# A two-layer hybrid backbone on one core: projections given out evenly between attention chunks, mask rows asked for three chunks ahead, the last MLP groups turned round

## The chip, the core and the metric

The kernel runs on one core of a Trainium2 chip. A core has five engines with instruction queues of their own: TensorE (PE, matrix products), VectorE (DVE), ScalarE (ACT), GpSimd (POOL) and SyncE (SP, which here issues nearly all DMAs). They meet through semaphores. The metric is device time in microseconds (us) of one execution; lower is better.

## What is computed

Two layers over 1024 latent tokens and 256 context tokens of width 1024, in fp32. Layer 0 mixes tokens by a short gated convolution, layer 1 by a bidirectional mLSTM with 8 heads. Each layer ends in an MLP with squared ReLU. The parts that matter here, cut:

```python
def _sqrelu_mlp(h, w1, w2):
    return jnp.square(jax.nn.relu(h @ w1)) @ w2

def body(carry, inp):                       # one chunk of 128 tokens of the mLSTM
    c_mat, n_vec, m = carry
    ...
    s = jnp.einsum('bhtd,bhsd->bhts', qc, kc) * jnp.exp(logd - m_t[..., None])
    w_inter = jnp.exp(inter - m_t)
    num = jnp.einsum('bhts,bhsv->bhtv', s, vc) + w_inter[..., None] * jnp.einsum('bhtd,bhdv->bhtv', qc, c_mat)
    den = jnp.sum(s, axis=-1) + w_inter * jnp.einsum('bhtd,bhd->bht', qc, n_vec)
    out = num / jnp.maximum(jnp.abs(den), jnp.exp(-m_t))[..., None]
    ...
    c_new = a[..., None, None] * c_mat + jnp.einsum('bhsd,bhsv->bhdv', kc * wk[..., None], vc)

def _mlstm_readout(h, o, norm_w, w_out):
    ...
    return (jax.nn.sigmoid(o) * h) @ w_out
```

The scan runs forwards and backwards in time, and both results are added.

## The kernel before

All large products are done in fp32 with operands split in a high and a low part, in three passes (`PASSES`); `split` (L109, L110) and `piece` (L122, L123) make the parts, each with one ScalarE cast and one VectorE subtraction. The order of work on each engine is made at build time by a list scheduler: an operation that stands earlier in the source has priority, but a later one may be put before it when the scheduler's own estimate says that the earlier one would wait. On the chip every engine then runs its list strictly in order.

**The MLP** (`mlp_up`, L488) uses a scheme with seven products for a two by two block product. For each of 16 steps `q` the weights are loaded and combined (`up_weights`), then `up_group` does a group of 84 products for the tokens of `A0` (384 of them a piece in layer 0, 256 in layer 1) and another for those of `A1`. A group's sums land in one tile `st7`, of which each pool has a single buffer (pool S1 for A0, pool M for A1), and one DMA stores it to `hid_d` (L469). `down_sums` (L471) loads the rows of the second weight matrix for a `k`, makes four differences on VectorE and stores them to `t_d`; it runs for `k = q - 2` at step `q`, and twice after the last step. `mlp_down` then reads `hid_d` (`hr`, L529; its pool lies over M's place), `w2` and `t_d`, casts and splits them, and does the down products `psd` (L536).

**The mLSTM** works through four pairs of heads (`Pair`, `j` 0 to 3). For a pair, `k`, `v` and `q` project the tokens (`psk`, `psv`, `psq`). `states` (L978) makes the state of each of 10 chunks (`pk`, `kk`, L982 to L998) and runs the recurrence over chunks on VectorE (L1002), for both directions at once. `attend` (L1006) then goes through 8 chunks for each head. A chunk's front (L1020 to L1040) makes the decay mask `Dm`: rows `nm_d` fetched to all partitions (one DMA per two chunks, two buffers), plus a triangular mask (L1026), exponential (L1032); it does the scores `po` (L1035) and their product with the mask, `pm` (L1039). A chunk's back multiplies with V and with the state (L1047, L1048, over `qw`, the queries times their decay, L1012) and normalises (L1052 to L1058) into `hb`. `out_gate` normalises a head (`rstd` on POOL, L241, L242, scaling L1070) and computes the gate (`pso`, sigmoid L1078); `read_out` transposes (`pth`, L1085), multiplies (L1087) and stores to `gd`, for all but the last two heads. `out_proj` (L353) loads those rows (`zt`), splits them (`zs`) and does the output products `op` (L371).

In the source the next pair's projections stand before `states` and `attend` of that pair as a whole; where they go on PE is the scheduler's choice.

Of the kernel before, what the change touches and what calls it, by code (L numbers as in the profile page):

```python
# [8 lines left out]
F32 = mybir.dt.float32  # L9
# [28 lines left out]
def hybrid_kernel(  # L38
# [449 lines left out]
    def mlp_up(l, As, sX, left, S1, acc):  # L488
# [317 lines left out]
    with ExitStack() as s1:  # L806
# [34 lines left out]
        class Pair:  # L841
# [12 lines left out]
            def k(self, groups, ps_pool=tp, tag="tp"):  # L854
                for t0, n in groups:
# [3 lines left out]

            def v(self, tiles):  # L860
                for t in tiles:
# [14 lines left out]
            def q(self, groups):  # L876
                w = load_w(wq[self.j])
                for t0, n in groups:
                    ps = tp.tile([P, 512], F32, tag="tp", name="psq")
                    mm_feat(ps[:, 0:n], w, t0, n)  # L880
# [4 lines left out]

        XG = ((256, 512), (768, 512))
        pair = Pair(0)
        pair.k(PG[0:2], acc, "acc")
        pair.v([0, 1, 2, 3, 4, 5, 7, 9])
        for f in pend:  # L890
            f(acc, "acc")
        pair.v([6, 8])
        gate_rows()
        pair.k(PG[2:])
        sT.close()
        with pool("gates", bufs=1, side="right") as gp:
# [60 lines left out]
            pair.q(XG)  # L957
            nxt = Pair(1)
            nxt.k(GROUPS)
# [18 lines left out]
        def states(pair):  # L978
            j = pair.j
            for c in range(NT):  # L980
# [9 lines left out]
                sb = 1 - c if c < NCT else NT + 1 - c  # L990
                for hh in range(2):
# [14 lines left out]
        def attend(pair, hh):  # L1006
            h = 2 * pair.j + hh
            kT, V, st = pair.kT, pair.V, sts[hh]
            qw = hp.tile([P, SEQ], F32, tag="qw", name="qw")
            for d, r in enumerate((lower, upper)):  # L1010
                nc.sync.dma_start(qw[r], w_d[d, h].partition_broadcast(64))
                nc.vector.tensor_mul(qw[r], qw[r], qz[hh * 64 : hh * 64 + 64, hh])  # L1012
            if pair.j < HEADS // 2 - 1:
                hb = hp.tile([P, 8, P], F32, tag="hb", name="hb")
            else:
                hb = pr.tile([P, 8, P], F32, tag="V" if hh else "kT", name="hb")
            ssq = small.tile([P, 8], F32, tag="ssq", name="ssq", bufs=4)
            Dm = {}

            def front(c):  # L1020
# [192 lines left out]
```

## Time and profile before

| | |
|---|---|
| time, median of 3 runs | 2582.22 us (2580.07 to 2582.91) |
| the profiled execution | 2577.89 us, of which the span of the profile is 2576.1 us |
| mean granted clock of TensorE | 0.989 of full |
| busy: PE, DVE, ACT, POOL | 97%, 64%, 44%, 4% of the span |
| chain that ended last | PE 53%, issue 30%, DVE 6%, DMA 6%, ACT 3%, POOL 2% |

PE is busy nearly always; that is a mean over stages, and "busy" says nothing of the clock. The part of the chain called issue is time in which an engine waited for nothing that the profile shows. The mLSTM stage is the stretch from about 1340 to 1860 us, the passages from the up to the down part of the MLP stand near 940 us (layer 0) and 2250 us (layer 1).

### The profile page before, as it was taken

Reading aid. Unit: us, or ns where it says so; the run is one execution under the profiler, and the core shown is the slowest. Engines: PE = TensorE matmul, PEld = TensorE weight load, DVE = VectorE, ACT = ScalarE, POOL = GpSimd, SP = SyncE. Lnnn points to the kernel's source line nnn. Section 1 sums busy time; section 2 is a strip of 40 time slices with the busy share of each in tenths; the row PEclk is TensorE's granted clock in tenths of the full one; section 3 lists DMA queues with packets and bytes.
Section 4 is the critical chain, followed back from the end, with each engine's and each line's share of the span. In section 5 each row is a group of like instructions: output and inputs, shape, how many; then the busy total and the mean of one; then the engine's idle time right before and its main releaser. Section 6 shows DMA issues by size and latency. Waiting matters only on the chain.

```text
span 2576.1 us, 38825 instructions
## 1 busy us (share of the span) xinstructions
PE 2488.1 (97%) x14520; PEld 2199.3 (85%) x14520; DVE 1651.6 (64%) x3058; ACT 1143.7 (44%) x2503; POOL 107.0 (4%) x229
## 2 busy tenths in 40 slices
PE   8999999999999999999999899999999999999998
PEld 5888887899999988888879788887789999978886
DVE  5777784687676664445864745546578787654565
ACT  5311112565445443334654444345456555444443
POOL 1000000100000000000111100000010000000010
PEclk9999999999999999999999899999999999999999
DMA  8456663436565676555751322222336777876675
GB/s 295 132 175 189 200 194 116 136 127 231 208 242 208 225 268 199 173 167 170 234 185 51 73 78 58 66 74 83 117 126 213 252 246 259 268 239 188 184 230 182
DMA packets 230207, 454.87 MB, mean 177 GB/s; under 512 B 17802, under 2 KB 109242, under 8 KB 230018
## 3 DMA queue, kind: packets, MB, share of 16 engines
q1 hardware_dynamic: 230018, 452.38, 54.2%
q8 instruction: 114, 1.87, 0.3%
q14 instruction: 75, 0.61, 0.1%
HBM read 326.78 MB, written 125.33 MB: 176 GB/s over the span
## 4 chain that ended last, share of the span: by engine, by line
PE 53%; issue 30%; DVE 6%; DMA 6%; ACT 3%; POOL 2%; DVEq 0%; POOLq 0%; SPq 0%; ACTq 0%
PE psd L536 12%; PE op L371 5%; PE psZ L433 4%; PE psW L433 4%; PE psX L433 4%; PE psv L865 3%; PE psc L129 3%; PE pso L129 3%; DMA Dm<-nm_d 3%; PE psb L129 3%; PE psu L129 3%; PE psY L433 2%; DMA mraw<-in_mod_w_dram 2%; PE psq L129 1%; DVE macc L220 1%
## 5 line engine op out<-in xcount | busy, mean ns | idle before, releaser
L536 PE MATMUL psd<-w,hp 128*128 128x512 f32 x3024 | 712.1, 397 | 10.8 <-ACT hp L530 10.8
L536 PEld LDWEIGHTS psd<-w,hp 128*128 128x128 f32 x3024 | 573.5, 190 | 145.7 <-ACT hp L530 11.9
L531 DVE TENSOR_TENSOR hp<-hr,hp 128x512 fp32r<-128x512 f32 (+1 forms) x226 | 169.4, 752 | 255.7 <-ACT hp L530 255.3
L530 ACT CAST hp<-hr 128x512 fp32r<-128x512 f32 (+1 forms) x226 | 151.1, 669 | 330.7 <-PE psd L536 278.0
L123 DVE TENSOR_TENSOR w<-raw,w 128x512 fp32r<-128x512 f32 x394 | 268.2, 685 | 40.9 <-ACT w L122 40.8
L122 ACT CAST w<-raw 128x512 fp32r<-128x512 f32 x394 | 242.5, 617 | 105.6 <-DMA raw<-in_w_dram 37.1
L433 PE MATMUL psX<-A,w 128*128 128x256 f32 (+1 forms) x1536 | 230.0, 298 | 2.2 <-ACT st L448 1.7
L433 PE MATMUL psZ<-A,w 128*128 128x256 f32 (+1 forms) x1536 | 226.8, 296 | 0.2 <-DVE st L452 0.2
L433 PE MATMUL psW<-A,w 128*128 128x256 f32 (+1 forms) x1536 | 226.8, 296 | 0.0
L433 PEld LDWEIGHTS psX<-A,w 128*128 128x128 f32 x1536 | 213.4, 189 | 3.4 <-ACT st L448 2.5
L433 PEld LDWEIGHTS psZ<-A,w 128*128 128x128 f32 x1536 | 211.9, 188 | 0.6 <-DVE st L452 0.5
L433 PEld LDWEIGHTS psW<-A,w 128*128 128x128 f32 x1536 | 211.8, 188 | 0.2 <-DVE st L454 0.2
L371 PE MATMUL op<-w,zs 128*128 128x512 f32 x864 | 206.1, 398 | 5.5 <-ACT zs L365 4.4
L371 PEld LDWEIGHTS op<-w,zs 128*128 128x128 f32 x864 | 162.5, 190 | 42.6 <-ACT zs L365 5.4
L463 ACT ACTIVATE st<-st 128x256 f32<-128x256 f32 (+1 forms) x192 | 85.2, 444 | 226.2 <-DVE st L454 159.0
L220 DVE SCALAR_TENSOR_TENSOR macc<-mraw,sil,macc 128x1024 f32<-128x1024 f32 x112 | 140.6, 1281 | 38.2 <-DMA mraw<-in_mod_w_dram 37.8
L109 ACT CAST w<-raw 128x1024 fp32r<-128x1024 f32 (+1 forms) x73 | 75.5, 1040 | 162.6 <-PE psc L129 61.6
L110 DVE TENSOR_TENSOR w<-raw,w 128x1024 fp32r<-128x1024 f32 (+1 forms) x73 | 87.8, 1209 | 78.7 <-ACT w L109 78.4
L865 PE MATMUL psv<-w,hT 128*128 128x256 f32 (+1 forms) x960 | 134.6, 294 | 0.5 <-ACT V L872 0.5
L865 PEld LDWEIGHTS psv<-w,hT 128*128 128x128 f32 x960 | 124.4, 192 | 1.1 <-ACT V L872 0.9
L433 PE MATMUL psY<-A,w 128*128 128x256 f32 (+1 forms) x768 | 116.0, 297 | 0.0
L129 PE MATMUL psc<-hT,w 128*128 128x512 f32 (+1 forms) x576 | 115.2, 352 | 0.6 <-DVE hT L279 0.4
(242 smaller groups left out, 3445.9 us busy)
## 6 DMA issues: line engine op xcount, KB each, us to landing
hid_d<-st SPq DMA_DIRECT2D x48, 896.0 KB, 5.1
mraw<-in_mod_w_dram SPq DMA_DIRECT2D x80, 512.0 KB, 4.0
raw<-in_w_dram SPq DMA_DIRECT2D x68, 512.0 KB, 3.8
hr<-hid_d SPq DMA_DIRECT2D x104, 320.0 KB, 3.7
rw<-in_w_dram SPq DMA_DIRECT2D x64, 512.0 KB, 5.7
raw<-t_d SPq DMA_DIRECT2D x128, 256.0 KB, 3.1
hr<-hid_d SPq DMA_DIRECT2D x122, 256.0 KB, 2.8
raw<-in_w_dram SPq DMA_DIRECT2D x96, 256.0 KB, 3.8
```

What stands on the lines that cost most here:

```text
L110: nc.vector.tensor_sub(w[1], src, w[0].bitcast(F32))
L122: nc.scalar.copy(w[:, 0], src)
L123: nc.vector.tensor_sub(w[:, 1], src, w[:, 0].bitcast(F32))
L129: nc.tensor.matmul(ps, w[a][:, k * P : (k + 1) * P], hold["hT"][:, k, b, t0 : t0 + n], start=(k == 0 and i == 0), stop=(k == KD - 1 and i ...
L220: nc.vector.scalar_tensor_tensor(ac[v], raw, s, ac[v], ALU.mult, ALU.add)
L371: nc.tensor.matmul(ps[h], zs[:, a, k, :], ws[k][b][:, h * 512 : (h + 1) * 512], start=(k == 0 and i == 0), stop=(k == KD - 1 and i == 2),)
L433: nc.tensor.matmul(ps, w[i][:, a, k * P : (k + 1) * P], A[:, PIECE[i], b, k, :], start=(first and k == 0 and j == 0), stop=(k == 3 and j = ...
L463: nc.scalar.activation(c, c, AF.Relu)
L530: nc.scalar.copy(h[:, 0], r)
L531: nc.vector.tensor_sub(h[:, 1], r, h[:, 0].bitcast(F32))
L536: nc.tensor.matmul(ps, h[:, a, o : o + P], w[:, b], start=(first and j == 0), stop=(last and j == 2))
L865: nc.tensor.matmul(ps[:, 0 : self.g], hold["hT"][:, k, a_, t * P : (t + 1) * P], self.wv[k // self.per][b_][:, k % self.per * self.g : (k ...
```

## The change

- `mlp_up`: steps 6 and 10 each do two `down_sums` in place of one, so that none is left after the last step. In the last step the group of A1 is done before that of A0.
- `k`, `v`, `q` and `out_gate` return lists of closures, one per PSUM tile (for `out_gate` half a tile). `Spread` calls them evenly over the steps of a loop. `states` gets, over its 10 steps, three `v` units of pair 1 for the first pair, later the gates and read-outs of the pair before (of its first head in the last pair). `attend` gets, over its 16 steps (both heads in one loop now), the other `v` and the `q` units of pair 1 (j = 0), the next pair's `k`, `v` and `q` (j = 1, 2), or the remaining gates, those of the last two heads too (j = 3).
- The mask rows come one chunk at a time (64 DMAs of 128 KB for 32 of 256 KB), in four buffers, asked for three chunks ahead, the first three before `states`; the mask is added in one operation per chunk, as many as before. The `qw` rows are asked for before `states`.
- After the last chunk only the read-outs of the last two heads are left.

```diff
@@ mlp_up
+            sums_due = 0
             for q in range(2, NQ):
                 w = up_weights(l, q, M)
-                down_sums(l, q - 2, M)
-                up_group(l, q, w, A0, n0, 0, S1, acc)
-                up_group(l, q, w, A1, n1, n0, M, acc)
-            down_sums(l, NQ - 2, M)
-            down_sums(l, NQ - 1, M)
+                for _ in range(2 if q in (6, 10) else 1):
+                    down_sums(l, sums_due, M)
+                    sums_due += 1
+                both = [(A0, n0, 0, S1), (A1, n1, n0, M)]
+                for A, n, c0, pl in both if q < NQ - 1 else both[::-1]:
+                    up_group(l, q, w, A, n, c0, pl, acc)
@@
+        class Spread:
+            def __init__(self, units, steps):
+                self.units, self.n, self.steps, self.done, self.i = units, len(units), steps, 0, 0
+
+            def __call__(self):
+                self.i += 1
+                while self.done * self.steps < self.i * self.n and self.done < self.n:
+                    self.units[self.done]()
+                    self.done += 1
@@ states
-        def states(pair):
+        def states(pair, step):
...
                 sb = 1 - c if c < NCT else NT + 1 - c
+                step()
                 for hh in range(2):
@@ attend
-                if c % 2 == 0:
-                    D2 = hp.tile([P, 2, 2 * P], F32, tag="Dm", name="Dm")
-                    nc.sync.dma_start(D2, nm_d[:, h, c * P : (c + 2) * P].partition_broadcast(P))
-                    for d in range(2):
-                        nc.vector.tensor_add(
-                            ch(D2[:, d]), ch(D2[:, d]), mask[:, d].unsqueeze(1).broadcast_to([P, 2, P])
-                        )
-                    Dm[c], Dm[c + 1] = D2[:, :, 0:P], D2[:, :, P : 2 * P]
+            def fetch(self, c):
+                D = hp.tile([P, 2, P], F32, tag="Dm", name="Dm", bufs=4)
+                nc.sync.dma_start(D, nm_d[:, self.h, c * P : (c + 1) * P].partition_broadcast(P))
+                self.Dm[c] = D
...
+                h, Dc = self.h, self.Dm[c]
+                nc.vector.tensor_add(Dc, Dc, mask)
...
-            nxt_ = front(0)
-            for c in range(8):
-                cur = nxt_
-                if c < 7:
-                    nxt_ = front(c + 1)
-                back(c, *cur)
+        def attend(pair, heads, step):
+            items = [(h, c) for h in heads for c in range(8)]
+            for h in heads:
+                h.begin()
+            nxt_ = heads[0].front(0)
+            for i, (hd, c) in enumerate(items):
+                cur = nxt_
+                if i + 3 < len(items):
+                    items[i + 3][0].fetch(items[i + 3][1])
+                if i + 1 < len(items):
+                    nxt_ = items[i + 1][0].front(items[i + 1][1])
+                step()
+                hd.back(c, *cur)
@@ the loop over pairs
-        fin = []
-        for j in range(HEADS // 2):
+        for j in range(NPR):
+            old = heads
             if j:
-                pair = nxt if j == 1 else Pair(j)
-                if j > 1:
-                    pair.k(GROUPS)
-                pair.v(all_tiles)
-                pair.q(XG)
-            if j < HEADS // 2 - 1:
-                for og, ro in fin:
-                    ro(og())
-                fin = []
-            states(pair)
-            fin += [attend(pair, hh) for hh in range(2)]
-        for og, ro in fin[:2]:
-            ro(og())
-        fin = fin[2:]
-        sgs = [og() for og, _ in fin]
-        for (_, ro), sg in zip(fin, sgs):
-            ro(sg)
+                pair = nxt
+            heads = [Head(pair, hh) for hh in range(2)]
+            for c in range(3):
+                heads[0].fetch(c)
+            if j == 0:
+                units = nxt.v(all_tiles) + nxt.q()
+                states(pair, Spread(units[0:3], NT))
+                units = units[3:]
+            else:
+                states(pair, Spread(rest(old if j < NPR - 1 else old[0:1]), NT))
+                if j < NPR - 1:
+                    nxt = Pair(j + 1)
+                    units = nxt.k(GROUPS) + nxt.v(all_tiles) + nxt.q()
+            if j == NPR - 1:
+                units = rest(old[1:2]) + heads[0].out_gate() + heads[1].out_gate()
+            attend(pair, heads, Spread(units, 16))
+        for hd in heads:
+            hd.read_out()
+        sgs = [hd.sg for hd in heads]
```

Three places show what the scheduler makes of it. The first is PE at the end of layer 0's up part: `A_3583` is A0 (384 columns), `A_4589` is A1 (256), the `w` are the combined weights of the last step. Before:

```order
2198 L433 MATMUL psZ<-A_3583,w_8644 128x384 x12
2199 L433 MATMUL psW<-A_3583,w_8648 128x384 x12
2200 L433 MATMUL psX<-A_4589,w_8626 128x256 x12
2201 L433 MATMUL psY<-A_4589,w_8632 128x256 x12
2202 L433 MATMUL psZ<-A_4589,w_8635 128x256 x12
2203 L433 MATMUL psW<-A_4589,w_8638 128x256 x12
2204 L433 MATMUL psX<-A_4589,w_8641 128x256 x12
2205 L433 MATMUL psZ<-A_4589,w_8644 128x256 x12
2206 L433 MATMUL psW<-A_4589,w_8648 128x256 x12
2207 L536 MATMUL psd<-w_8931,hp 128x512 x15
```

After:

```order
2196 L433 MATMUL psW<-A_4589,w_8662 128x256 x12
2197 L433 MATMUL psX<-A_3583,w_8650 128x384 x12
2198 L433 MATMUL psY<-A_3583,w_8656 128x384 x11
2199 L433 MATMUL psX<-A_4589,w_8665 128x256 x12
2200 L433 MATMUL psZ<-A_4589,w_8668 128x256 x12
2201 L433 MATMUL psW<-A_4589,w_8672 128x256 x12
2202 L433 MATMUL psY<-A_3583,w_8656 128x384
2203 L433 MATMUL psZ<-A_3583,w_8659 128x384 x12
2204 L433 MATMUL psW<-A_3583,w_8662 128x384 x12
2205 L433 MATMUL psX<-A_3583,w_8665 128x384 x12
2206 L433 MATMUL psZ<-A_3583,w_8668 128x384 x12
2207 L433 MATMUL psW<-A_3583,w_8672 128x384 x12
```

A1's first four products now come before A0's, its other three are put in after two of A0, and the rest of A0 is the last work before the down products.

The second is SyncE's queue at the same place: `hid_d<-st` is the store of a group, `hr<-hid_d` the first loads of the down part, `rw` and `t_d` belong to `down_sums`. Before:

```order
238 L476 DMA rw<-in_w_dram 128x1024
239 L469 DMA hid_d<-st_8663 128x7x384
240 L476 DMA rw<-in_w_dram 128x1024
241 L529 DMA hr<-hid_d 128x640 x3
242 L469 DMA hid_d<-st_8771 128x7x256
243 L484 DMA t_d<-t_8895 128x512
244 L485 DMA t_d<-rw 128x512
```

After:

```order
242 L486 DMA t_d<-rw 128x1024
243 L469 DMA hid_d<-st_8536 128x7x256
244 L523 DMA raw_9029<-in_w_dram 128x512
245 L531 DMA hr<-hid_d 128x640 x3
246 L523 DMA raw_9054<-in_w_dram 128x512
247 L469 DMA hid_d<-st_8687 128x7x256
248 L531 DMA hr<-hid_d 128x640 x3
```

The loads of the sums are gone from here, `hr` is asked for earlier, and the stores of the last two groups stand behind the first loads or right ahead of them.

The third is PE in the attention of pair 1. `L1035` (after: L1065) is the score product of a front, `L1047` and `L1048` (after: L1078, L1079) are the products of a back, `psv` a projection for the next pair. Before, two backs of the second head and what stands between them:

```order
3270 L1047 MATMUL po<-V,pm 128x129
3271 L1048 MATMUL po<-st_12979,qw 128x129
3272 L1047 MATMUL po<-V,pm 128x129
3273 L1048 MATMUL po<-st_12979,qw 128x129
3274 L865 MATMUL psv<-w_14395,hT 128x256
3275 L865 MATMUL psv<-w_14396,hT 128x256
3276 L865 MATMUL psv<-w_14395,hT 128x256 x2
3277 L1047 MATMUL po<-V,pm 128x129
3278 L1048 MATMUL po<-st_12979,qw 128x129
3279 L1047 MATMUL po<-V,pm 128x129
3280 L1048 MATMUL po<-st_12979,qw 128x129
3281 L865 MATMUL psv<-w_14396,hT 128x256
```

After, the back of a chunk, the front of the next but one, and the beginning of one unit (24 projections), after which the next back comes:

```order
3205 L1078 MATMUL po<-V,pm 128x129
3206 L1079 MATMUL po<-st_12978,qw 128x129
3207 L1078 MATMUL po<-V,pm 128x129
3208 L1079 MATMUL po<-st_12978,qw 128x129
3209 L1065 MATMUL po<-qz,kT 128x128
3210 L869 MATMUL psv<-w_14083,hT 128x256
3211 L869 MATMUL psv<-w_14084,hT 128x256
3212 L869 MATMUL psv<-w_14083,hT 128x256 x2
```

Where two to five projections stood between backs, with a long unbroken run of them later, one whole unit now stands in every step.

## Rows read from the trace of the kernel before

**Rows 1.** waits of PE, 1340:1860 us: engine, line waited, us in total, times, longest

```profile
PE po L1035 <- DVE hb L1057: 15.3, 10, 2.1
PE po L1047 <- DVE pm L1039: 6.0, 6, 1.9
```

**Rows 2.** waits of VectorE (DVE), the same stretch

```profile
DVE Dm L1026 <- DMA Dm<-nm_d: 40.2, 23, 3.5
```

**Rows 3.** windows: stretch, its length, engines' busy us, PEclk, DMA share, GB/s

```profile
1450.00:1500.00 50.00, 43.00 (x319) 41.00 (x318) 33.27 (x107) 28.09 (x113) 3.85 (x5) 0.93 0.33 64
1470.00:1490.00 20.00, 15.96 (x105) 15.36 (x105) 11.19 (x43) 11.16 (x49) 1.86 (x2) 0.83 0.46 81
1560.00:1590.00 30.00, 24.02 (x194) 22.57 (x193) 17.85 (x68) 19.42 (x84) 1.98 (x3) 1.00 0.46 104
1670.00:1710.00 40.00, 33.03 (x266) 31.35 (x265) 19.80 (x71) 23.11 (x99) 3.67 (x4) 1.00 0.36 83
1760.00:1790.00 30.00, 24.12 (x155) 20.90 (x155) 17.92 (x65) 20.92 (x73) 1.86 (x2) 0.94 0.18 54
```

**Rows 4.** timeline of PE, 1580:1636: start, us, work, count, [idle before <-releaser]

```profile
1584.55 0.49 PE L1047 MATMUL po<-V,pm 128*128 128x129 f32 x2 [0.81 <-DVE pm L1039]
...
1585.46 23.89 PE L865 MATMUL psv<-w,hT 128*128 128x256 f32 x197
1609.20 11.31 PE L129 MATMUL psq<-hT,w 128*128 128x512 f32 x48
```

**Rows 5.** timeline of PE, layer 0, end of the up part

```profile
924.17 2.28 PE L433 MATMUL psW<-A,w 128*128 128x384 f32 x12
...
934.83 1.58 PE L433 MATMUL psW<-A,w 128*128 128x256 f32 x12
940.87 19.47 PE L536 MATMUL psd<-w,hp 128*128 128x512 f32 x71 [4.45 <-ACT hp L530]
```

**Rows 6.** timeline of PE, layer 1, start of the down part

```profile
2248.35 5.49 PE L536 MATMUL psd<-w,hp 128*128 128x512 f32 x12 [3.97 <-ACT hp L530]
2256.19 19.02 PE L536 MATMUL psd<-w,hp 128*128 128x512 f32 x74 [2.35 <-ACT hp L530]
```

**Rows 7.** windows behind the two passages

```profile
940.00:950.00 10.00, 9.13 (x28) 7.08 (x29) 4.24 (x7) 2.98 (x5) 0.00 (x0) 0.66 1.02 349
2248.00:2264.00 16.00, 13.30 (x39) 10.03 (x40) 7.51 (x11) 4.15 (x8) 0.00 (x0) 0.70 0.92 300
```

**Rows 8.** groups of VectorE, 1340:1860: busy us, mean ns, idle before

```profile
L1002 DVE SCALAR_TENSOR_TENSOR st<-st,adb 128x258 f32<-128x258 f32 x64 | 27.7, 482 | 0.4
...
L1026 DVE TENSOR_TENSOR Dm<-Dm,mask 128x256 f32<-128x256 f32 x64 | 25.5, 420 | 40.3 <-DMA Dm<-nm_d 40.2
L998 DVE COPY st<-pk 64x129 f32<-64x129 f32 x80 | 22.3, 295 | 6.4 <-ACT st L997 4.3
...
L985 DVE TENSOR_TENSOR kk<-pk,wkcol 128x128 f32<-128x128 f32 x80 | 20.2, 287 | 12.0 <-PE pk L982 8.7 <-PE pk L993 1.2 <-DMA w_d<-msk 0.5
L1012 DVE TENSOR_TENSOR qw<-qw,qz 64x1024 f32<-64x1024 f32 x16 | 19.5, 1219 | 0.4
```

**Rows 9.** DMA issues, 1340:1860: KB each, median us to landing

```profile
Dm<-nm_d SPq DMA_DIRECT2D x32, 256.0 KB, 5.3
```

**Rows 10.** timeline of SyncE's queue, 905:950

```profile
930.92 0.37 SPq L469 DMA_DIRECT2D hid_d<-st  x1
...
936.45 1.27 SPq L529 DMA_DIRECT2D hr<-hid_d  x3
```

**Rows 11.** timeline of PE, end of the mLSTM stage

```profile
1790.86 22.09 PE L129 MATMUL pso<-hT,w 128*128 128x512 f32 x94
...
1817.37 2.07 PE L371 MATMUL op<-w,zs 128*128 128x512 f32 x4 [2.68 <-ACT zs L365]
```

**Rows 12.** timeline of VectorE, the same place

```profile
1796.31 1.29 DVE L1070 TENSOR_TENSOR hb<-hb,rstd 128x512 f32<-128x512 f32 x2 [2.51 <-POOL rstd L242]
```

**Rows 13.** the page, part 6: DMA issues, KB each, us to landing

```profile
hid_d<-st SPq DMA_DIRECT2D x48, 896.0 KB, 5.1
```

More of the change, by code (lines that the diff above doesn't have):

```diff
@@ L854, in k, with unit @@
             def k(self, groups, ps_pool=tp, tag="tp"):
-                for t0, n in groups:
+                def unit(t0, n):
                     ps = ps_pool.tile([P, 512], F32, tag=tag, name="psk")
@@ L858, in k, with unit @@
                     nc.scalar.copy(self.kT[:, t0 : t0 + n], ps[:, 0:n])
+                return [lambda g=g: unit(*g) for g in groups]
             def v(self, tiles):
-                for t in tiles:
+                def unit(t):
                     ps = tp.tile([P, 512], F32, tag="tp", name="psv")
@@ L874, in v, with q, unit @@
                         nc.scalar.copy(gcol[:, t, :, 0:8], ps[:, 256:GP].rearrange("p (g c) -> p g c", g=4))
-            def q(self, groups):
-                w = load_w(wq[self.j])
-                for t0, n in groups:
+                return [lambda t=t: unit(t) for t in tiles]
+            def q(self):
+                w = {}
+                def unit(t0, n):
+                    if not w:
+                        w[0] = load_w(wq[self.j])
                     ps = tp.tile([P, 512], F32, tag="tp", name="psq")
-                    mm_feat(ps[:, 0:n], w, t0, n)
+                    mm_feat(ps[:, 0:n], w[0], t0, n)
                     for hh, r in enumerate((lower, upper)):
@@ L884, in q, with run @@
                         )
+                return [lambda g=g: unit(*g) for g in XG]
+        def run(units):
+            for u in units:
+                u()
+        class Spread:
[6 more added lines that the diff above has]
+                    self.done += 1
         XG = ((256, 512), (768, 512))
         pair = Pair(0)
-        pair.k(PG[0:2], acc, "acc")
-        pair.v([0, 1, 2, 3, 4, 5, 7, 9])
+        run(pair.k(PG[0:2], acc, "acc"))
+        run(pair.v([0, 1, 2, 3, 4, 5, 7, 9]))
         for f in pend:
             f(acc, "acc")
-        pair.v([6, 8])
+        run(pair.v([6, 8]))
         gate_rows()
-        pair.k(PG[2:])
+        run(pair.k(PG[2:]))
         sT.close()
@@ L1040, in front, with back @@
                 return po, pm
-            def back(c, po, pm):
+            def back(self, c, po, pm):
                 g = c + NCT
@@ L1046, in back @@
                 for d in range(2):
-                    nc.tensor.matmul(o[:, d], pm[:, d], V[:, g, hh], start=True, stop=False)
+                    nc.tensor.matmul(o[:, d], pm[:, d], self.pair.V[:, g, self.hh], start=True, stop=False)
                     nc.tensor.matmul(
-                        o[:, d], qw[:, c * P : (c + 1) * P], st[:, steps[d], d], start=False, stop=True
+                        o[:, d], self.qw[:, c * P : (c + 1) * P], sts[self.hh][:, steps[d], d], start=False, stop=True
                     )
```

82 lines of the change are left out of this document (50 added, 32 removed).

## The prediction

> **What bounds the kernel now.** TensorE (PE) sets the end, so I looked for the places where it waits or runs at its lower clock, and read each from the stage it stands in.
>
> First the waits of PE in the mLSTM stage, 1340 to 1860 us. Two lines carry nearly all: the score product of a chunk waits for VectorE's `hb`, 15.3 us, and the back of a chunk for the masked scores `pm`, 6.0 us [rows 1]. Behind both stands VectorE, and what VectorE waits for is the mask rows: 40.2 us in 23 waits [rows 2]. The windows then say where. In the second half of each of the four pairs PE is busy for only 43.00 of 50 us, 24.02 of 30, 33.03 of 40 and 24.12 of 30: 7.0 + 6.0 + 7.0 + 5.9 = 25.8 us idle. In the first and the last of them the granted clock is 0.93 and 0.94: 43.00 x 0.07 + 24.12 x 0.06 = 4.4 us more [rows 3]. So at most 30.2 us can be won there. The timeline shows why filling is possible: the back of a chunk stands 0.81 us for `pm`, and less than a microsecond after the last back PE gets 197 projections for the next pair in one unbroken piece of 23.89 us, then 48 of another kind in 11.31 us [rows 4]. Work that could have filled the holes stands behind them.
>
> Second, the passage from the MLP's up to its down part. In layer 0 PE ends its last up product, begun at 934.83, and starts again at 940.87 after 4.45 us [rows 5]; in layer 1 it stands 3.97 and 2.35 us [rows 6]. After that it runs slowly: in the ten microseconds from 940 the clock is 0.66 with 9.13 us busy, in the sixteen from 2248 it is 0.70 with 13.30 us busy [rows 7]. The first is 9.13 x 0.34 = 3.1 us lost, the second 13.30 x 0.30 = 4.0. Together 4.45 + 3.1 + 3.97 + 2.35 + 4.0 = 17.9 us.
>
> **Part 1: spread projections and masks fetched ahead.** PE's instructions are the same; only their places change. Per step (one chunk of one head) PE gets one unit of work or a little less. A 256-wide projection takes 23.89/197 = 0.121 us, a 512-wide one 11.31/48 = 0.236 [rows 4]; the ten small matmuls of a chunk cost about 1.3 us (estimate: 319 matmuls in 43.00 us, 0.135 each [rows 3]). In pairs 1 and 2 fifteen units stand over sixteen steps: 240 x 0.121 + 120 x 0.236 = 57 us, so 3.6 + 1.3 = 4.9 us a step. In pair 0: (168 x 0.121 + 48 x 0.236)/16 = 2.0, so 3.3. In pair 3: 144 x 0.236/16 = 2.1, so 3.4. The mask add of VectorE is 0.42 us a chunk [rows 8] and its other four operations are small, so PE is the longest in each step, and `pm` is asked for one step ahead. The mask rows were fetched with two buffers, so that a transfer could start only when a chunk pair was done with, and landed 5.3 us later [rows 9]. Now they start three steps ahead, 9.9 us in the shortest pair. 32 DMAs become 64 of half the size, with runs of 512 bytes instead of 1 KB. I price one at the old 5.3 us: still covered. The cost of issuing is on SyncE's queue, 1.27/3 = 0.42 us each [rows 10], against steps of over 3 us.
>
> The Trainium skill ("DMA: Bandwidth & Descriptors", Specifications) puts the smallest transfer for line rate at 512 bytes, so the new runs are just on it, and its section on the anatomy of one DMA gives about 2.0 us fixed plus bytes/436e3 on GpSimd's path: by it (an estimate) 64 fetches would take 64 x 2.3 = 147 us where 32 took 32 x 2.6 = 83. The row's 5.3 us for 256 KB is twice that page's figure, so the row decides; the page speaks against the change only where fetches are not overlapped.
>
> What is late next? The first back of a pair needs the recurrence of the states, all on VectorE: 27.7 + 22.3 + 20.2 us over four pairs [rows 8], 17.6 a pair, and both heads' `qw` products, 19.5/4 = 4.9, now together ahead of the first back: 22.4 us. Counted in the order, PE has ahead of the first whole back 144 projections (17.4 us) and some 60 small matmuls in pair 0, 96 + 35 (30.9 us) in pairs 1 and 2, 72 (17.0 us) in pair 3; before it was 132 (16.0), 46 (10.9), 46 (10.9) and 48 (11.3). So the cover has grown everywhere and about fits. I leave 4 us of residual stall (bounds 0, if all is covered, and 12, four times 3).
>
> The end of the stage loses cover. Before, 94 `pso` products, 22.09 us, stood between the last back and the last transposes, and PE then stood 2.68 us at the output projection [rows 11]. Now they stand inside pair 3's attention, and the last read-out hangs on a chain: the sum of squares, POOL's rstd and 1.29 us of scaling on VectorE, which before waited 2.51 us for rstd [rows 12]. That is about 2.2 (estimate: the same order as the rstd wait) + 2.5 + 1.3 = 6 us, newly exposed. But before lost at this place too, behind `zs`, and those loads move up with the read-outs of the older heads. I take +2 us (bounds 0 and +6).
>
> Two more activation table loads on ScalarE, which is at most 19.42/30 = 65% busy there [rows 3], I cost at nothing; without that cover they would come under the residual.
>
> Sum of part 1: -30.2 + 4 + 2 = -24 us (bounds -30 and -12).
>
> **Part 2: the MLP.** The down part's first load, `hr`, was issued at 936.45, when the last A1 product had released the pool it lies over [rows 10], and PE began 4.4 us later [rows 5]. Now A1 is done first. Behind it PE has the rest of A0, 61 matmuls of 384 columns in layer 0: 61 x 2.28/12 = 11.6 us [rows 5], and about 50 x 1.58/12 = 6.6 us in layer 1. Both exceed 4.4, so the first wait and with it the low clock go. The second wait of layer 1 came from `hr` loads queued behind the weights and stores of the last two sums; these are gone from the end. Gain 17.9 us.
>
> The price is a new wait. A1's last group now follows directly on A1's group of q=14, and the one `st7` buffer of pool M must be stored before ScalarE's first copy into it. The store goes out 930.92 - 926.45 = 4.5 us after a group's last matmul [rows 5, 10] and lands 5.1 us later [rows 13]: 9.6 us. Ahead of the product that needs ScalarE's copy PE has four groups of A1 and 24 matmuls of A0: 4 x 1.58 + 2 x 2.28 = 10.9 us in layer 0, 6 x 1.58 = 9.5 in layer 1, each about 0.9 less since successive rows overlap by 0.16 [rows 5]. I take 0.6 and 1.0 us; bounds 0 and 4 each (no cover in the last product, or a store landing late under a full DMA share).
>
> The sums moved to q=6 and q=10 double the DVE and DMA work of two rounds in each layer. A doubled sum is four operations of 1.29/2 = 0.65 us [rows 12], so 2.6 us; four such rounds, 10.4 us if nothing hides them. PE shows no wait at all in the rounds of layer 0 shown [rows 5], so VectorE has slack; I take 1 us (bounds 0 and 10).
>
> Sum of part 2: -17.9 + 1.6 + 1 = -15 us (bounds -18 and 0).
>
> **Together** -39 us, rounded to -40 since the smaller terms were rounded up. The profiled execution is 2577.89 us; 2537.9 after. The median of the runs shown is 4.3 us above it, so 2542 us.
>
> **Rivals.**
> - (a) The attention gains nothing: the fetches stay late. It needs a landing time over 9.9 us, double the row's. For it: twice as many DMAs, and qw and weight loads in one queue; against it: a DMA share of 0.18 to 0.46 in the holes [rows 3]. Then only part 2 and the tail: 2582 - 15 + 2 = 2569 at worst, 2566 with the clock part kept. Chance 0.12.
> - (b) The passages gain nothing: the store of `st7` lands late (4 us each) and the doubled sums show (10 us). For it: a DMA share of 1.02 and 0.92 at just this place [rows 7]. Then 2582 - 24 = 2558. Chance 0.17.
> - (c) Slower: PE's clock. The steps now alternate a dense unit with small matmuls for 16 x (3.3 + 2 x 4.9 + 3.4) = 264 us. If the clock stays at the 0.83 shown from 1470 to 1490 [rows 3], that costs 264 x 0.2 = 53 us: 2582 - 40 + 53 = 2595. It decides from a mean clock of 0.85, where the cost passes 45 us. Against it: from 1560 to 1590, with a fifth of the time idle, the clock was 1.00. Chance 0.04.
> - (d) Neither gain: list scheduling had already filled what could be filled, and the holes only move. Then 2580. For it: the same engines do the same work; against it: the unbroken pieces of [rows 4]. Chance 0.05.
>
> **How the numbers follow.** The forecast, 2542, has 0.60, with its own range 2533 to 2553; 0.02 are left for more than all of the bounds. The range 2532 to 2567 leaves out (c), (d) and half of (a) or less, about 0.15. A difference of 0.2%, 5 us, is about what a measurement here can tell from no change. Faster: 0.60 + 0.12 + 0.17 + 0.02 = 0.91; same 0.05 from (d); slower 0.04 from (c).
>
> **What would show it.** Right: VectorE's wait for `Dm` under 10 us, PE idle in the four attention stretches under 12 us, PE going from up to down products with a gap under 1.5 us and a clock of 1.00 in both layers, a wait of ScalarE's `st7` copy near 1 us, and 4 to 6 us of waits before the last transposes. Wrong: `Dm` landing in over 9 us, PE waiting in the first back of each pair for the recurrence, or the gap before `psd` replaced by one inside A0's last group.

## The result, and the profile after

The changed kernel took 2606.05 us (median of 4 runs, 2602.68 to 2613.82) against 2581.14 us before: ratio 1.010, 95% interval 1.0077 to 1.0124. It is slower by about 25 us where 40 us less was forecast. The profiled execution has a span of 2600.9 us, 24.8 more than before.

The MLP part did what was forecast. The page's group of the down products shows no idle time, where the two passages of before had 4.45, 3.97 and 2.35 us [rows 5, 6]:

```profile
L538 PE MATMUL psd<-w,hp 128*128 128x512 f32 x3024 | 705.0, 395 | 0.0
```

The timeline of PE in layer 0 (start, us, work, idle before) shows the end of A0's group running straight into the down products, and the new store wait ahead of A1's fifth product (`psX`), 0.72 us:

```profile
918.24 1.69 PE L433 MATMUL psX<-A,w 128*128 128x256 f32 x12 [0.72 <-ACT st L448]
...
931.23 2.27 PE L433 MATMUL psW<-A,w 128*128 128x384 f32 x12
933.34 12.01 PE L538 MATMUL psd<-w,hp 128*128 128x512 f32 x51
```

The loss is in the mLSTM stage. The waits of PE from 1340 to 1910 us (us in total, times, longest):

```profile
PE po L1078 <- DVE pm L1070: 34.4, 20, 4.6
PE pk L1021 <- DVE kk L1012: 10.0, 3, 5.4
```

From 1430 us to the last back the window (PE busy us second, clock third from the end) is

```profile
1430.00:1840.00 410.00, 360.00 (x2215) 314.09 (x2214) 203.15 (x583) 168.36 (x544) 14.84 (x16) 0.95 0.22 59
```

so 50.0 us idle and 360 x 0.05 = 18 us to the clock. Before, the two largest waits were 15.3 and 6.0 us [rows 1]; now the back of a chunk waits for its product with the mask, `pm`, for 34.4 us, and the states wait for VectorE's `kk`. What VectorE waits for:

```profile
DVE Dm L1060 <- DMA Dm<-nm_d: 118.3, 50, 4.5
```

That is three times the 40.2 us of [rows 2], in twice as many waits. The fetches themselves are not slower than before; the source view of L1054 has

```profile
DMA to landing us min/median/max: 4.3/4.7/6.4
```

against a median of 5.3 us for one of double the size [rows 9]. The Trainium skill's fixed cost plus bytes ("DMA: Bandwidth & Descriptors", on the anatomy of one DMA, given for GpSimd's path: about 2.0 us plus bytes/436e3) has the form of this, a small part for the bytes, but not the size: by it (an estimate) the two would take 2.3 and 2.6 us, and the trace has about twice that.

How one chunk goes in pair 2 stands in four timelines. VectorE (L1060 is the mask add, L1070 the product with the mask, L1084 a step in the normalising of the chunk before):

```profile
1706.82 0.42 DVE L1070 TENSOR_TENSOR pm<-po,Dm 128x256 f32<-128x256 f32 x1
...
1711.80 0.42 DVE L1060 TENSOR_TENSOR Dm<-Dm,mask 128x256 f32<-128x256 f32 x1 [3.70 <-DMA Dm<-nm_d]
1713.04 0.16 DVE L1084 TENSOR_TENSOR dn<-dn,flcol 128x2 f32<-128x2 f32 x1 [0.81 <-ACT dn L1083]
1713.12 0.41 DVE L1070 TENSOR_TENSOR pm<-po,Dm 128x256 f32<-128x256 f32 x1
```

ScalarE, the exponentials of the same chunk:

```profile
1712.26 0.69 ACT L1062 ACTIVATE Dm<-Dm,acol 128x128 f32<-128x128 f32 x2 [3.46 <-DVE Dm L1060]
```

SyncE's queue, the fetch that this add waits for, and the next one:

```profile
1707.30 0.36 SPq L1054 DMA_DIRECT2D Dm<-nm_d  x1
...
1713.59 0.36 SPq L1054 DMA_DIRECT2D Dm<-nm_d  x1
```

PE (L1078 begins a back, L869 is the unit given out to the step):

```profile
1707.29 0.49 PE L1078 MATMUL po<-V,pm 128*128 128x129 f32 x2 [1.47 <-DVE pm L1070]
...
1708.85 3.12 PE L869 MATMUL psv<-w,hT 128*128 128x256 f32 x24 [0.17 <-ACT V L876]
1713.59 0.49 PE L1078 MATMUL po<-V,pm 128*128 128x129 f32 x2 [1.62 <-DVE pm L1070]
```

Read them together. At 1707.30 the fetch is issued, the moment the product of four chunks earlier (1706.82) has freed its buffer. It lands at about 1711.8, and there VectorE's add begins, after 3.70 us of idle time. The product for the back that PE stands at comes behind it, at 1713.12, and PE goes on at 1713.59, after 1.62 us. In between VectorE waits 0.81 us for a `dn` of ScalarE, which stands behind the exponentials of the chunk just added: ScalarE's list has been drawn ahead in the same way. The product frees the next buffer, the next fetch is issued at 1713.59, and so on: one chunk in 6.3 us, 1707.30 to 1713.59, of which the fetch is 4.5. PE's own work in that time is a back of 1.0 us, a score product and a unit of 3.1 us.

The order of VectorE's rows says why the add stands there. With A for the add and P for the product of chunk number n (counted over all 64), VectorE's list in pair 2 reads, for the changed kernel and for the first experiment on it:

```
changed:  A42 P39 A43 P40 A44 P41 A45 P42 A46 P43 A47
pinned:   A42 P42 A43 P43 A44 P44 A45 P45 A46 P46 A47
```

In the changed kernel A44 stands ahead of P41, though in the source it comes behind P43. A44 needs a buffer that P40 frees. So the four buffers and the fetch three chunks ahead give next to no lead: each add waits out nearly a whole fetch in front of the product that PE waits for.

Between the pairs the same thing holds up the states. The add for the next pair's fourth chunk, whose buffer the last product of the pair before frees, stands ahead of the `kk` that PE waits for (from pair 1 to pair 2; `kk` follows at 1631.47):

```profile
1627.91 0.42 DVE L1060 TENSOR_TENSOR Dm<-Dm,mask 128x256 f32<-128x256 f32 x1 [4.29 <-DMA Dm<-nm_d]
```

### The profile page after: what moved, and what is told of

Its sections match the earlier page's. It is cut to its first block, busy times and chain, and to the rows that moved or that the text cites. A ratio compares the mean times of both kernels' runs of the same rounds, so it can differ in the third digit from the quotient of the medians.

```text
span 2600.9 us, 38779 instructions
## 1 busy us (share of the span) xinstructions
PE 2492.7 (96%) x14520; PEld 2199.7 (85%) x14520; DVE 1653.6 (64%) x3058; ACT 1145.9 (44%) x2505; POOL 108.6 (4%) x229
## 4 chain that ended last, share of the span: by engine, by line
PE 44%; issue 29%; DMA 12%; DVE 9%; ACT 4%; POOL 2%; DVEq 0%; POOLq 0%; SPq 0%; ACTq 0%
PE psd L538 11%; DMA Dm<-nm_d 7%; PE op L371 5%; PE psZ L433 4%; PE psW L433 4%; PE psX L433 4%; PE psc L129 3%; DMA mraw<-in_mod_w_dram 3%; PE psb L129 2%; PE psu L129 2%; PE psY L433 2%; PE pso L1103 2%; PE psv L869 1%; DVE macc L220 1%; POOL rstd L242 1%
## 5 line engine op out<-in xcount | busy, mean ns | idle before, releaser
L538 PE MATMUL psd<-w,hp 128*128 128x512 f32 x3024 | 705.0, 395 | 0.0
L869 PE MATMUL psv<-w,hT 128*128 128x256 f32 (+1 forms) x960 | 133.1, 294 | 2.3 <-ACT V L876 1.9
L869 PEld LDWEIGHTS psv<-w,hT 128*128 128x128 f32 x960 | 124.3, 194 | 4.6 <-ACT V L876 4.1
L1103 PE MATMUL pso<-hT,w 128*128 128x512 f32 x384 | 113.5, 435 | 0.0
```

Of the source, the lines that this page charges most:

```text
L538: nc.tensor.matmul(ps, h[:, a, o : o + P], w[:, b], start=(first and j == 0), stop=(last and j == 2))
L869: nc.tensor.matmul(ps[:, 0 : self.g], hold["hT"][:, k, a_, t * P : (t + 1) * P], self.wv[k // self.per][b_][:, k % self.per * self.g : (k ...
L1103: nc.tensor.matmul(self.po, self.wo[a][:, k * P : (k + 1) * P], hold["hT"][:, k, b, t0 : t0 + 512], start=(k == 0 and n == 0), stop=(k == ...
```

## The experiments

**The loop: pin the add, widen the fetch, move the add.** The theory: the loop of fetch, add and product above costs the time. Rival one: the small transfers are too slow. Rival two: the units given out by hand make PE wait. `e2_pin` changes one call, which puts the add on VectorE behind all that stands before it in the source; the scheduler then arranges the rest around it anew:

```diff
-                nc.vector.tensor_add(Dc, Dc, mask)
+                tc.keep_in_program_order(nc.vector.tensor_add(Dc, Dc, mask))
```

> The changed kernel with one thing different: the mask add of a chunk is pinned on VectorE behind everything that stands before it in the source, so that it can't be moved ahead of the products of earlier chunks. Same transfers, same buffers, same units. Theory of the loop (VectorE's add waits for a fetch, the fetch for a buffer that is freed by a product queued behind the add): the loop opens, VectorE's wait for masks falls from 118 us to under 30, the four attention stretches from 286 us to under 240, time 2545 to 2570. Rival one (the small transfers themselves are too slow or too many): the waits stay, 2595 to 2610. Rival two (the units spread by hand make PE wait): 2595 or more, with PE waiting elsewhere than for the product with the mask.

Measured: 2545.81 us, ratio to before 0.9882 (0.9867 to 0.9896), 60 us below the changed kernel by the medians, 56 by the two ratios. VectorE's waits for mask rows, 118.3 us, are gone from the list of its waits (under 30 were expected). The wait of PE for the product, and the first and last weight load of a back in pair 1 (the columns behind the count are ns minimum, median, maximum):

```profile
PE po L1078 <- DVE pm L1070: 5.5, 4, 1.7
```

```profile
L1078 PEld LDWEIGHTS po<-V,pm x64: 187/192/192, 1526.8 to 1595.0; 128*128 128x128 f32 x64
```

The same row of the changed kernel, and of before, where a pair's projections stood outside:

```profile
L1078 PEld LDWEIGHTS po<-V,pm x64: 186/191/338, 1537.3 to 1623.8; 128*128 128x128 f32 x64
```

```profile
L1047 PEld LDWEIGHTS po<-V,pm x64: 186/192/192, 1546.2 to 1585.1; 128*128 128x128 f32 x64
```

Pair 1's attention went from 86.5 to 68.2 us with the same transfers, buffers and units given out. All four pairs, by the same rows, went from 52.8 + 86.5 + 87.6 + 57.4 = 284.3 us to 47.3 + 68.2 + 68.3 + 61.4 = 245.2, a little over the 240 expected: the last pair got longer, which is taken up below. Another 20 us came between the pairs, where the stretches from the last back to the next pair's first went from 113.3 to 93.3 us by the same rows, and PE no longer waits for `kk`. From 1430 us to the last back the window is now

```profile
1430.00:1783.00 353.00, 342.13 (x2234) 304.48 (x2234) 211.16 (x593) 188.46 (x561) 14.80 (x16) 0.99 0.28 73
```

10.9 us idle and 3.4 to the clock, where the changed kernel lost 50.0 and 18. Both rivals fail: neither the transfers nor the units given to a step were touched in the source.

`e3_wide` leaves the order to the scheduler and fetches two chunks at once, so that a round of the loop carries two:

```diff
+                if c % 2:
+                    return
-                D = hp.tile([P, 2, P], F32, tag="Dm", name="Dm", bufs=4)
-                nc.sync.dma_start(D, nm_d[:, self.h, c * P : (c + 1) * P].partition_broadcast(P))
-                self.Dm[c] = D
+                D = hp.tile([P, 2, 2 * P], F32, tag="Dm", name="Dm", bufs=2)
+                nc.sync.dma_start(D, nm_d[:, self.h, c * P : (c + 2) * P].partition_broadcast(P))
+                self.Dm[c], self.Dm[c + 1] = D[:, :, 0:P], D[:, :, P : 2 * P]
```

> The changed kernel with the mask rows fetched for two chunks at once into two buffers, the bytes of buffer the same as with four small ones; the scheduler stays free. Theory of the loop: its round of landing, add and product (6.2 us a chunk) now carries two chunks, 6.7/2 = 3.4 us a chunk, less than PE needs in pairs 1 and 2 (4.4), so these run at PE's pace, and pairs 0 and 3 nearly; 2560 to 2578. Rival one (number of transfers): a gain too, of the same kind. Rival two (units): no gain, 2600 or more.

Measured: 2556.43 us, ratio 0.9922 (0.9907 to 0.9937), 4 us below the expected range. Pair 1 runs at the pinned kernel's pace, although VectorE still waits 70.5 us for masks:

```profile
L1080 PEld LDWEIGHTS po<-V,pm x64: 187/192/192, 1539.4 to 1607.8; 128*128 128x128 f32 x64
```

```profile
DVE Dm L1062 <- DMA Dm<-nm_d: 70.5, 27, 5.4
```

So within a pair the wait costs little when its round is no longer than PE's work for the chunks that it carries. The 10 us to the pinned kernel are lost between the pairs, where the stretches are 109.9 us against 93.3 and PE still waits for `kk`, with an add ahead of it:

```profile
PE pk L1021 <- DVE kk L1012: 11.3, 3, 5.9
```

`e17_wide_pin` takes both edits:

> The changed kernel with the pinned add and the mask rows fetched for two chunks at once into two buffers. If the size and number of transfers cost nothing by themselves, the time is that of the pinned kernel with small ones, ratio 0.986 to 0.990. Rival (the small transfers do cost): 4 us or more below it, ratio under 0.9865. The other way: with two buffers of two chunks the lead is shorter by up to one step, and the waits for masks come back in part, ratio over 0.990.

Measured: 2545.91 us, ratio 0.9884 (0.9862 to 0.9906), the same as with small transfers. No cost of their size and number can be seen once nothing stands behind them.

`e5_pool` gives the add to GpSimd (`nc.gpsimd.tensor_add`).

> The changed kernel with the mask add given to GpSimd, whose queue holds little else; fetches, buffers and units as in the changed kernel. Theory of the loop: the wait for a fetch no longer stands in front of VectorE's products, so the time falls to 2550 to 2575, unless GpSimd's add takes over 2 us. Rival one (transfers): the product still waits for its mask, through GpSimd: 2595 to 2610. Rival two (units): 2600 or more.

Measured: 2608.23 us, ratio 1.0121 (1.0106 to 1.0137): no gain, against what the loop theory had expected. By the time alone the run would speak for one of the rivals. The waits of ScalarE and of VectorE show where it went, and the pair is as slow as in the changed kernel:

```profile
ACT Dm L1062 <- POOL Dm L1060: 125.0, 50, 4.4
```

```profile
DVE dn L1084 <- ACT dn L1083: 116.3, 33, 6.3
```

```profile
L1078 PEld LDWEIGHTS po<-V,pm x64: 186/192/337, 1542.4 to 1629.6; 128*128 128x128 f32 x64
```

ScalarE's exponential needs the add's result and had been drawn ahead too, so now ScalarE stands 125.0 us, with its work on earlier chunks behind, and VectorE waits 116.3 us for that work. In the changed kernel ScalarE had stood nearly as long, behind VectorE's add:

```profile
ACT Dm L1062 <- DVE Dm L1060: 105.3, 38, 4.3
```

By this reading the loop had only changed its engine. To see whether that is so, `e16_pool_pin` pins the exponentials on ScalarE in the same way:

> The kernel with the mask add on GpSimd, and the two exponentials of a chunk pinned on ScalarE behind everything that stands before them in the source. Theory of the loop, now through ScalarE: in the run with GpSimd alone ScalarE waited 125 us for the adds with its work on earlier chunks behind; pinned, that goes, and the time falls to 2545 to 2560, ratio 0.988 to 0.993. Rival (the fetches are late whoever waits): 2595 or more, ratio over 1.008.

Measured: 2560.94 us, ratio 0.9938 (0.9917 to 0.9960), just above the range, and far from the rival's 2595. GpSimd still waits 271.2 us for fetches, but nothing of earlier chunks stands behind it, and pair 1 is back at 69 us:

```profile
L1060 POOL TENSOR_TENSOR Dm<-Dm,mask 128x256 f32<-128x256 f32 x64 | 52.6, 824 | 282.1 <-DMA Dm<-nm_d 271.2 <-DVE pm L1072 3.7 <-DVE dn L1086 3.1
```

```profile
L1080 PEld LDWEIGHTS po<-V,pm x64: 186/192/193, 1533.2 to 1602.4; 128*128 128x128 f32 x64
```

The rest to the pinned kernel, 15 us, I did not take apart; the add is 0.82 us here against 0.42 on VectorE.

**Did before have the loop too?** `e8_before_pin` is the kernel before with its mask adds pinned, nothing else.

> The kernel before with only its mask adds pinned on VectorE, nothing spread. If before's holes in the attention came from the same loop (adds ahead of products), 8 to 20 us faster than before, ratio 0.992 to 0.997. If they came from missing filler for PE, within 5 us of before or slower, ratio 0.998 to 1.005.

Measured: 2563.96 us, ratio 0.9948 (0.9933 to 0.9963). VectorE's wait for masks, 40.2 us in [rows 2], is now

```profile
DVE Dm L1026 <- DMA Dm<-nm_d: 6.8, 4, 2.3
```

The run is about 13 us faster by the ratio, and the two waits of PE in [rows 1] have fallen from 21.3 to 12.2 us (1400 to 1900 us):

```profile
PE po L1035 <- DVE hb L1057: 8.5, 5, 2.0
PE po L1047 <- DVE pm L1039: 3.7, 3, 1.3
```

So about 13 of the 30.2 us (25.8 idle, 4.4 of the clock) that I read as missing filler were the same loop, with two chunks a round.

**The MLP part and its halves.** `e1_mlp` is before with only the MLP edit.

> The kernel before with only the change in the MLP's up part (sums moved to steps 6 and 10, A1's group first in the last step). All theories put the loss into the mLSTM stage, so this alone should gain: no wait before the first down product in either layer, about 18 us less than before less 1 to 3 us for the new store wait: 2562 to 2567 us. A rival says that the doubled sums or the store wait eat it: then within 5 us of before, 2576 to 2586.

Measured: 2558.32 us, ratio 0.9929 (0.9916 to 0.9942), 18 us, against 2575.99 for before in the same comparison; that is 4 us below the range expected. In layer 0:

```profile
931.08 2.27 PE L433 MATMUL psW<-A,w 128*128 128x384 f32 x12
933.19 27.11 PE L538 MATMUL psd<-w,hp 128*128 128x512 f32 x116
```

`e9_turn` turns the groups and leaves the two sums at the end; `e10_sums` moves the sums and leaves the groups (cut; on the left against before, on the right against the changed kernel's source):

```diff
# e9_turn                                          # e10_sums
-  up_group(l, q, w, A0, n0, 0, S1, acc)           +  for A, n, c0, pl in both:
-  up_group(l, q, w, A1, n1, n0, M, acc)           -  for A, n, c0, pl in both if q < NQ - 1 else both[::-1]:
+  both = [(A0, n0, 0, S1), (A1, n1, n0, M)]
+  for A, n, c0, pl in both if q < NQ - 1 else both[::-1]:
+      up_group(l, q, w, A, n, c0, pl, acc)
```

> The kernel before with only the groups of the last MLP step turned round; the two last sums stay at the end. The first wait before the down products (4.45 and 3.97 us with the slow clock behind it) goes, the second one of layer 1 (2.35 us, loads queued behind those of the sums) stays: 10 to 14 us faster than before, ratio 0.9945 to 0.996. Rival: the sums still standing at the end hold the queue that issues the loads, so that little is gained: ratio over 0.997.

> The kernel before with only the sums moved to steps 6 and 10; the groups of the last step stay in their order. The second wait of layer 1 (2.35 us and the slow clock behind it) goes, the first ones stay: 3 to 8 us faster, ratio 0.997 to 0.999. Rival: the doubled steps cost what the end gains: 1.000 or above.

Measured: 2564.62 us, 0.9950 (0.9934 to 0.9967), for the turn; 2572.36 us, 0.9989 (0.9979 to 0.9999), for the sums, at the small end of what was expected. The waits of PE at layer 1's passage are, with the turn alone and with the sums alone,

```profile
PE psd L537 <- ACT hp L531: 3.0, 2, 2.2
PE psd L537 <- ACT p L545: 1.4, 1, 1.4
```

```profile
PE psd L538 <- ACT hp L532: 4.1, 1, 4.1
```

The turn is worth 13 us; the sums moved alone leave the first wait and are worth 3. 13 + 3 = 16 of the 18 us that both give.

**The end of the stage.** In the pinned kernel PE loses most of what is left at the end of pair 3. The window (busy us of PE second, clock third from the end) and PE's timeline behind the last chunk:

```profile
1760.00:1800.00 40.00, 25.23 (x110) 21.00 (x111) 23.23 (x56) 22.72 (x59) 1.83 (x2) 0.71 0.39 116
```

```profile
1787.75 1.94 PE L1125 MATMUL pth<-ident,hb 128*128 128x128 f32 x8 [4.70 <-DVE hb L1119]
1790.75 1.22 PE L371 MATMUL op<-w,zs 128*128 128x512 f32 x2 [1.05 <-ACT zs L365]
1795.21 35.03 PE L371 MATMUL op<-w,zs 128*128 128x512 f32 x140 [3.25 <-DVE zs L366]
```

40 - 25.23 = 14.8 us idle, and 25.23 x 0.29 = 7.3 us to the clock. `e6_tail48` and `e7_tail24` emit the last head's gate, or its second half, behind the attention, as cover:

```diff
-                units = rest(old[1:2]) + heads[0].out_gate() + heads[1].out_gate()
+                units = rest(old[1:2]) + heads[0].out_gate()
...
+        run(heads[1].out_gate())
         for hd in heads:
             hd.read_out()
```

> The kernel with the pinned add, and the last head's gate (48 products, 11.3 us) put back behind the last chunk, as cover for the last read-outs. If the cover was what the end of the stage lacks (PE stood 5.3 us before the last transposes, 1.05 and 3.25 us at the output projection, and ran slowly from 1760 to 1800, 21.6 us in all with the pinned add), most of that comes back: 8 to 14 us below the pinned kernel, ratio to before 0.983 to 0.986. Rival: the gates are missed as filler in the last pair's attention, which loses as much as the end gains: ratio 0.987 to 0.990.

> As the run before, with only half of the last head's gate (24 products, 5.7 us) behind the last chunk. The chain to be covered is about 6 us, so by the theory of the cover it gains nearly as much, 6 to 12 us below the pinned kernel. Rival as for the run before.

Measured: 2542.50 us, 0.9866 (0.9849 to 0.9883), and 2544.82 us, 0.9876 (0.9860 to 0.9893): at most 4 us below the pinned kernel, with overlapping intervals, where 6 to 14 were expected. The scheduler had drawn the gates forward all the same, as PE's timeline of the first shows:

```profile
1777.14 0.80 PE L1078 MATMUL po<-V,pm 128*128 128x129 f32 x2 [4.05 <-DVE pm L1070]
...
1786.50 1.94 PE L1125 MATMUL pth<-ident,hb 128*128 128x128 f32 x8 [4.70 <-ACT w L109]
```

The last back still waits 4.05 us and the transposes 4.70, with nothing between them (in the second run the transposes wait the same 4.70 us). So these two runs did not test the cover. `e14_stay24` and `e15_stay48` leave a half or the whole of the gate behind the attention too, and pin the gates' products of pair 3 in their steps on PE:

```diff
+                            if hold.get("late"):
+                                tc.keep_in_program_order(mm)
...
+            hold["late"] = j == NPR - 1
             attend(pair, heads, Spread(units, 16))
```

> The kernel with the pinned add, in which the gates of the last pair's attention are pinned on PE too, in the step in which they are given out, and the second half of the last head's gate (24 products, 5.7 us) stands behind the last chunk. In the earlier tries the scheduler had drawn the gates forward, so that nothing covered the end. Theory of the cover: the 21.6 us lost between 1760 and 1800 shrink to about 10, 8 to 14 us below the pinned kernel, ratio to before 0.983 to 0.986. Rival: what holds the end is VectorE and ScalarE themselves (split of the output weights, masks, normalising), so that the order on PE changes little: ratio 0.986 to 0.989.

> As the run before, with the whole gate of the last head (48 products, 11.3 us) behind the last chunk. Theory of the cover: as good or up to 4 us better, since the output projection's own waits (1.05 and 3.25 us) are covered too. Rival: the gates are missed in the last steps of the attention, 2 to 6 us worse than with 24.

Measured: 2540.59 us, 0.9865 (0.9850 to 0.9881), with 24 products at the end, and 2549.36 us, 0.9894 (0.9880 to 0.9909), with 48. With 24:

```profile
1760.00:1800.00 40.00, 31.25 (x145) 25.93 (x144) 21.16 (x46) 23.96 (x56) 1.83 (x2) 0.83 0.50 152
```

```profile
1777.89 6.37 PE L1103 MATMUL pso<-hT,w 128*128 128x512 f32 x24
1784.10 1.04 PE L1127 MATMUL pth<-ident,hb 128*128 128x128 f32 x8
1789.68 15.53 PE L371 MATMUL op<-w,zs 128*128 128x512 f32 x53 [4.54 <-ACT zs L365]
```

In these 40 us PE is busy 6 us longer and the clock is 0.83 in place of 0.71; the wait before the transposes is gone, the one before the output projection has grown to 4.54 us. The loss in the window goes from 22.1 to 8.75 + 31.25 x 0.17 = 14.1 us, where about 10 was expected. What is left there is in part ScalarE's: the last backs still wait 4.21 us, and in that time ScalarE loads a table (ACT_TABLE_LOAD) ahead of the exponentials that they need:

```profile
1774.38 0.80 PE L1078 MATMUL po<-V,pm 128*128 128x129 f32 x2 [4.21 <-DVE pm L1070]
```

```profile
1771.88 1.28 ACT L1062 ACT_TABLE_LOAD   x1
1773.17 0.69 ACT L1062 ACTIVATE Dm<-Dm,acol 128x128 f32<-128x128 f32 x2
```

With 48 it is worse by 9 us in the median, more than the rival's 2 to 6; that the last steps miss them is likely but was not taken apart. Half the gate at the end is worth about 4 us over the pinned kernel by the ratios, whose intervals overlap; the ratio, 0.9865, lies in the rival's range and not in that of the cover. So the end is only in part a matter of cover.

**What the spread is worth.** `e13_pin_mlp` is before with its adds pinned and the MLP edit, nothing spread.

> The kernel before with the MLP part of the change and its own mask adds pinned, nothing spread by hand. If the two gains are in places apart they add: 0.9929 and 0.9948 give 0.9877, the same as the spread kernel with the pinned add (0.9882), and the hand spread is worth nothing here. Rival: the spread is worth 5 us or more beside the pin, and this run stands at 0.990 or above.

Measured: 2548.49 us, 0.9890 (0.9877 to 0.9904). The two gains add as far as the interval tells (the 0.9877 that was expected lies at its edge), and the hand spread with a pinned add (0.9882) is the same within the intervals. What the spread fills in the steps it gives back at the end. In the attention of pairs 1 and 2 PE is idle 0.07 us each with it and 3.2 us each without. From pair 3's first back to the output projection it is idle 15.3 us, at a clock of 0.91, with it (1720.6 to 1850 us), and 9.4 us, at 0.97, without (1722.8 to 1840 us). The fastest version that was run is `e14_stay24`, 1.35% below before, with `e6_tail48` the same within the intervals.

## Why the prediction was wrong

**The step that failed** is in part 1, "Now they start three steps ahead, 9.9 us in the shortest pair". The lead was counted in the source, between a fetch and its own chunk. On the chip a fetch starts when its buffer is free, with the product of four chunks earlier, and the add that waits for it stood three products ahead of its place on VectorE. The lead that counts is from the product that frees the buffer to the next product that stands behind the add: one chunk, with a fetch of about 4.5 us inside. The prediction read the order on PE and on SyncE's queue and took VectorE's for the source's ("`pm` is asked for one step ahead"); VectorE's rows would have shown it. In the loop a chunk took 6.3 us where the sum had 4.9. By the ratios of the changed kernel (1.010) and of the MLP part alone (0.9929) part 1 cost about 44 us where -24 was forecast.

**Rival (a)** named the place and the wrong mechanism. Its condition, a landing of over 9.9 us, is not met, and the sign that was named for it, a landing of over 9 us, did not come either: the longest was 6.4. It allowed only for a lost gain, and the result is 37 us above its worst case, 2569. That a wait in an in-order queue makes a loop with a period of its own, and can be longer than what it replaces, was in none of the rivals. **Rival (c)**, the slower one, asked for the clock; from 1500 to 1900 us the windows of 100 us show 0.91 to 0.97, and the pin cured the loss without touching the units. The clock cost 18 us from 1430 to 1840 us, against 50.0 of idle time, and went back to 0.99 when the waits went.

**The mask adds of before.** That the holes, 30.2 us with the clock, were missing filler was half wrong: pinning alone gives 13 us. The other half was right for pairs 1 and 2, where the spread with a pinned add leaves 0.07 us idle each.

**What late next.** "The first back of a pair needs the recurrence": this cover held; in the pinned kernel PE waits 5.5 us for all products with the mask together.

**The tail**, +2 us (bounds 0 and +6), was mis-sized. In the pinned kernel 14.8 + 7.3 = 22 us are lost from 1760 to 1800. Before, the window over its last chunks and the start of the output projection is

```profile
1780.00:1840.00 60.00, 54.34 (x265) 44.56 (x264) 29.93 (x61) 23.86 (x62) 3.52 (x7) 0.94 0.43 138
```

60 - 54.34 = 5.7 us idle and 54.34 x 0.06 = 3.3 to the clock, 9 us; so the term is about +13. The windows take in pair 3's last chunks on both sides; of the 22 us about 9 lie before the last back's end at 1782.9. The wait before the last transposes, 4.70 us, is within the 4 to 6 that were forecast, and the output projection's waits, 1.05 + 3.25, are little more than before's 2.68 + 1.03; the chunks ahead, from which the scheduler had drawn the gates away, and the low clock were not counted.

**The table loads**, priced at nothing. In the changed kernel there are two more, 13 for 11, as counted; in the pinned kernel there are 24 of 1.28 us, 13 of them from 1720 to 1800 us, and some stand in the chain that PE waits for at the end, as shown for `e14_stay24`. No run took them apart.

**Part 2** was right in mechanism and nearly in size: -15 forecast, -18 measured alone; the store wait is 0.72 us in layer 0 (0.6 forecast) and does not show in layer 1 (1.0 forecast). The 0.6 did not follow from its own terms: 10.9 - 0.9 = 10.0 us of cover against 9.6 leaves no wait. In the rounds of the doubled sums PE waits at most 0.9 us for VectorE (1 forecast).

With the loop open the time comes out nearly as forecast, 2546 for 2542, but by luck: the gain is 30 us of the 40, and before ran 5 us faster in the later comparisons. Part 1 gave 12 us of its 24, about as much as the pin gives without any spreading, and part 2 gave 3 more than its 15.

## What to carry to other kernels

A prefetch's lead is not its distance in the source. Follow the loop on every engine: what frees the buffer, what stands in the queue of the engine that waits for the transfer, and what the freeing instruction waits for; if the waiting instruction stands ahead of it, buffers and early issue give little, and the period is the transfer's latency and the work from its landing to the freeing of the buffer (here 4.5 and 1.8 of 6.3 us). Where a list scheduler sets the order, read its rows for the engine that waits for the DMA, and pin that instruction; moving it to an idle engine helped here only when the engine that takes its result was pinned too.

## What was not expected of the hardware

A broadcast of 128 KB in runs of 512 bytes lands nearly as late (4.7 us) as one of 256 KB in runs of 1 KB (5.3 us [rows 9]), so a fetch of half the size pays nearly the same latency. And a queue with 271 us of waits (GpSimd's in `e16_pool_pin`) can stand in a kernel that is 0.6% faster than before, while one with 118.3 us (VectorE's) stood in one that was 1% slower: what counts is what stands behind the wait.
